# A FiLM layer on one core: one slab of 128 rows per partition instead of four of 32

## The chip, the core and the metric

The kernel runs on one core of a Trainium2 chip. The metric is the device time of one execution in microseconds, a median of several.

The engines are named as in the profile: PE multiplies matrices (PEld loads its weights), DVE is the vector engine, ACT the scalar engine, POOL is GpSimd, and SP issues DMAs and waits; DVEq or ACTq is the part of an engine that issues. The SBUF is the core's memory on the chip. A DMA is split into packets over 16 DMA engines; a completion packet of 4 bytes reports that an engine has done its part. A semaphore is the counter that such a report raises and that an instruction waits for. All times within an execution are counted from the start of the profile's span.

## The reference

```python
# x: (32, 512, 256), conditioning: (32, 64), gamma_proj, beta_proj: (64, 256), float32
gamma = conditioning @ gamma_proj
beta = conditioning @ beta_proj
return (x * (1 + gamma[:, None, :]) + beta[:, None, :]).astype(np.float32)
```

This layer scales and shifts each row by a gamma and a beta that depend on the batch. Some 16.8 MB are read, 16.8 MB are written, and each element gets one multiplication and one addition.

## The kernel before

x is cut into 4 slabs. In a slab each of the 128 partitions holds 32 consecutive rows of 256 numbers; all slabs stay in the SBUF. Loads are issued by SP, stores by ACT. The stores are held back until most loads have landed: ACT first reads one number of the last but one load (`held`, called the hold below). Of every 16 rows DVE computes 11 and POOL 5.

```python
    SLABS = 4
    BS = batch // SLABS            # batches in a slab
    REP = P // BS                  # partitions that share a batch
    ROWS = BS * seq // P           # rows per partition in a slab: 32
    x_v = x.flatten_outer_dims().rearrange("(s p r) d -> s p r d", s=SLABS, p=P)
    ...
    LOADS = {0: [8, 8, 8, 8], 3: [26, 6]}
    STORES = {0: (32,), 1: (32,), 2: (32,), 3: (16, 32)}
    GROUP = 16
    ON_DVE = 11
    ...
    nc.scalar.dma_start(out=gbproj[0::2, :], in_=gamma_proj)
    nc.scalar.dma_start(out=gbproj[1::2, :], in_=beta_proj)
    ...
    for s in range(SLABS):         # gamma and beta of a slab's 128 partitions
        for h in range(2):
            nc.tensor.matmul(p_t[:, h * dim : (h + 1) * dim],
                             lhsT=cond_T[h][:, s * P : (s + 1) * P], rhs=gbproj, ...)
        # ACT copies 1 + gamma and beta to the SBUF, for POOL
    ...
                nc.vector.scalar_tensor_tensor(out=v, in0=rows(g_p, nv), scalar=1.0, in1=v,
                                               op0=ALU.add, op1=ALU.mult)
                nc.gpsimd.tensor_tensor(out=w, in0=w, in1=rows(g_s, nw), op=ALU.mult)
                nc.vector.tensor_add(out=v, in0=v, in1=rows(b_p, nv))
                nc.gpsimd.tensor_tensor(out=w, in0=w, in1=rows(b_s, nw), op=ALU.add)
                if s == 0 and r0 + GROUP == ROWS:
                    # the hold: ACT reads a number of the last but one load before it issues any store
                    nc.scalar.copy(out=held, in_=slabs[-1][:, LOADS[SLABS - 1][0] - 1, 0:1])
                for e0, e1 in zip((0,) + STORES[s], STORES[s]):
                    if r0 < e1 <= r0 + GROUP:
                        nc.scalar.dma_start(out=o_v[s, :, e0:e1, :], in_=xs[:, e0:e1, :])
```

Of the kernel before, what the change touches and what calls it, by code (L numbers as in the profile page):

```python
# [2 lines left out]

# [5 lines left out]


@with_exitstack
def kernel(
    ctx: ExitStack,
    tc: tile.TileContext,
    x: bass.AP,
    conditioning: bass.AP,
    gamma_proj: bass.AP,
    beta_proj: bass.AP,
    out: bass.AP,  # L20
):
    nc = tc.nc
    f32 = mybir.dt.float32
    ALU = mybir.AluOpType

    batch, seq, dim = x.shape
    cond_dim = conditioning.shape[1]
    P = 128
    SLABS = 4
    BS = batch // SLABS  # L30
    REP = P // BS
    ROWS = BS * seq // P
    assert SLABS * BS == batch and REP * BS == P and ROWS * REP == seq

    x_v = x.flatten_outer_dims().rearrange("(s p r) d -> s p r d", s=SLABS, p=P)
    o_v = out.flatten_outer_dims().rearrange("(s p r) d -> s p r d", s=SLABS, p=P)

    LOADS = {0: [8, 8, 8, 8], 3: [26, 6]}
    STORES = {0: (32,), 1: (32,), 2: (32,), 3: (16, 32)}
    GROUP = 16  # L40
    ON_DVE = 11

    consts = ctx.enter_context(tc.tile_pool(name="consts", bufs=1))
    xpool = ctx.enter_context(tc.tile_pool(name="xpool", bufs=1))
    psum = ctx.enter_context(tc.tile_pool(name="psum", bufs=1, space=bass.MemoryType.PSUM))


    cond_s = consts.tile([batch, cond_dim], f32)
    nc.scalar.dma_start(out=cond_s, in_=conditioning)  # L49

    gbproj = consts.tile([2 * cond_dim, dim], f32)
    nc.scalar.dma_start(out=gbproj[0::2, :], in_=gamma_proj)  # L52
    nc.scalar.dma_start(out=gbproj[1::2, :], in_=beta_proj)

    slabs = []
    for s in range(SLABS):
        xs = xpool.tile([P, ROWS, dim], f32, name=f"xs{s}")
        slabs.append(xs)
        r = 0
        for n in LOADS.get(s, [ROWS]):  # L60
            nc.sync.dma_start(out=xs[:, r : r + n, :], in_=x_v[s, :, r : r + n, :])
            r += n
        assert r == ROWS


    ident = consts.tile([batch, batch], f32)
    make_identity(nc, ident)
    rident = consts.tile([batch, batch * REP], f32)
    nc.vector.tensor_copy(  # L69
        out=rident.rearrange("p (b g) -> p b g", g=REP),  # L70
        in_=ident.to_broadcast([batch, batch, REP]),
    )


    cond_T = []
    for h in range(2):
        wide = consts.tile([batch, cond_dim, 2], f32, name=f"wide{h}")
        nc.vector.memset(wide, 0.0)  # L78
        nc.vector.tensor_copy(out=wide[:, :, h], in_=cond_s)  # L79
        t_p = psum.tile([2 * cond_dim, batch * REP], f32, name=f"cond_T_p{h}")  # L80
        nc.tensor.matmul(t_p, lhsT=wide.rearrange("b k h -> b (k h)"), rhs=rident,  # L81
                         start=True, stop=True)
        t_s = consts.tile([2 * cond_dim, batch * REP], f32, name=f"cond_T{h}")
        nc.vector.tensor_copy(out=t_s, in_=t_p)  # L84
        cond_T.append(t_s)

    gb_p, gb_s = [], []
    for s in range(SLABS):
        p_t = psum.tile([P, 2 * dim], f32, name=f"gb_p{s}")
        for h in range(2):  # L90
            nc.tensor.matmul(p_t[:, h * dim : (h + 1) * dim],  # L91
                             lhsT=cond_T[h][:, s * P : (s + 1) * P], rhs=gbproj,
                             start=True, stop=True)
        s_t = consts.tile([P, 2 * dim], f32, name=f"gb_s{s}")
        nc.scalar.activation(out=s_t[:, :dim], in_=p_t[:, :dim],  # L95
                             func=mybir.ActivationFunctionType.Identity,
                             bias=1.0, scale=1.0)
        nc.scalar.copy(out=s_t[:, dim:], in_=p_t[:, dim:])  # L98
        gb_p.append(p_t)
        gb_s.append(s_t)  # L100

    def rows(t, n):
        return bass.AP(tensor=t.tensor, offset=t.offset, ap=[t.ap[0], [0, n], t.ap[1]])

    held = consts.tile([P, 1], f32)
    with tc.manual_schedule():
        for s in range(SLABS):
            xs = slabs[s]
            g_p, b_p = gb_p[s][:, :dim], gb_p[s][:, dim:]
            g_s, b_s = gb_s[s][:, :dim], gb_s[s][:, dim:]  # L110
            for r0 in range(0, ROWS, GROUP):
                v = xs[:, r0 : r0 + ON_DVE, :]
                w = xs[:, r0 + ON_DVE : r0 + GROUP, :]
                nv, nw = ON_DVE, GROUP - ON_DVE
                nc.vector.scalar_tensor_tensor(out=v, in0=rows(g_p, nv), scalar=1.0, in1=v,  # L115
                                               op0=ALU.add, op1=ALU.mult)
                nc.gpsimd.tensor_tensor(out=w, in0=w, in1=rows(g_s, nw), op=ALU.mult)  # L117
                nc.vector.tensor_add(out=v, in0=v, in1=rows(b_p, nv))  # L118
                nc.gpsimd.tensor_tensor(out=w, in0=w, in1=rows(b_s, nw), op=ALU.add)  # L119
                if s == 0 and r0 + GROUP == ROWS:  # L120

                    nc.scalar.copy(out=held, in_=slabs[-1][:, LOADS[SLABS - 1][0] - 1, 0:1])  # L122

                for e0, e1 in zip((0,) + STORES[s], STORES[s]):
                    if r0 < e1 <= r0 + GROUP:
                        nc.scalar.dma_start(out=o_v[s, :, e0:e1, :], in_=xs[:, e0:e1, :])
            assert STORES[s][-1] == ROWS


# [1 line left out]
_INS = ['x', 'conditioning', 'gamma_proj', 'beta_proj']  # L131
_OUTS = [((32, 512, 256), 'float32')]


# [23 lines left out]
```

## Time and profile before

| | before |
|---|---|
| time, median of the first 3 runs | 84.08 us |
| profiled span | 82.4 us |
| DVE busy, POOL busy | 51.1 us, 46.4 us |
| loads of x on q1, rest on q10, share of 16 engines | 48.3%, 48.1% |
| first DVE instruction on x, last one ends | 12.81 us, 61.9 us |
| first store issued | 41.08 us |

The lines behind this table are shown and read in the prediction below. It is enough here to see that two kinds of work share the span: arithmetic, which is over at 61.9 us, and transfers, which fill all of it.

Two lines of the timeline that the prediction uses without showing (start, duration, engine, line, operation, operands, the idle time before it and what ended it):

```profile
9.19 5.66 PE L91 MATMUL gb_p<-gbproj,cond_T 128*128 128x256 f32 x16 [0.59 <-DMA gbproj<-in_beta_proj_dram]
...
12.81 3.09 DVE L115 SCALAR_TENSOR_TENSOR xs<-gb_p,xs 128x2816 f32<-128x2816 f32 x1 [3.48 <-ACT gb_s L98]
```

The projections gate PE, and gamma and beta gate the first instruction on x.

### The profile page before, as it was taken

How to read it: one execution, taken by the hardware profiler on the slowest of the kernel's cores; microseconds unless marked ns; L12 is line 12 of the kernel's file. 1: busy time of each engine (PE TensorE's matmuls, PEld its weight loads, DVE VectorE, ACT ScalarE, POOL GpSimd, SP SyncE). 2: the span in 40 equal slices, each digit the busy share in tenths (PEclk: the TensorE clock that was granted, in tenths of full speed). 3: DMA queues.
4: the chain of work that ended last, by engine and by line, in shares of the span. 5: the costliest groups of instructions: out<-in, count | busy, mean ns of one | idle time of the engine just before them, and what ended most of it. 6: DMA issues, size and time to landing. Idle time of an engine off the chain costs nothing.

```text
span 82.4 us, 180 instructions
## 1 busy us (share of the span) xinstructions
PE 9.4 (11%) x20; PEld 5.5 (7%) x20; DVE 51.1 (62%) x23; ACT 4.1 (5%) x10; POOL 46.4 (56%) x22
## 2 busy tenths in 40 slices
PE   0069799200000000000000000000000000000000
PEld 0041478000000000000000000000000000000000
DVE  1023307999999999999999999999990000000000
ACT  0600017400000000000000000000000000000000
POOL 2000008999999999999999999999600000000000
PEclk9999999998555555555555555555555555555555
DMA  3899999979979998999797996996995999789992
GB/s 52 322 417 426 429 425 541 461 318 493 493 334 445 509 397 370 439 465 452 301 564 318 509 493 270 509 493 270 509 509 254 509 509 429 334 382 493 397 397 111
DMA packets 2080, 33.69 MB, mean 409 GB/s; under 512 B 288, under 2 KB 416, under 8 KB 544
## 3 DMA queue, kind: packets, MB, share of 16 engines
q1 hardware_dynamic: 1152, 16.78, 48.3%
q10 hardware_dynamic: 928, 16.92, 48.1%
HBM read 16.92 MB, written 16.78 MB: 409 GB/s over the span
## 4 chain that ended last, share of the span: by engine, by line
DVE 43%; issue 17%; DMA 9%; PE 4%; ACTq 1%; ACT 1%
DVE xs L115 30%; DVE xs L118 13%; DMA gbproj<-in_beta_proj_dram 9%; PE gb_p L91 4%; ACTq L52 1%; ACTq L49 0%; ACT gb_s L95 0%; ACT gb_s L98 0%
## 5 line engine op out<-in xcount | busy, mean ns | idle before, releaser
L117 POOL TENSOR_TENSOR xs<-xs,gb_s 128x1280 f32<-128x1280 f32 x8 | 23.1, 2889 | 11.5 <-ACT gb_s L95 11.5
L115 DVE SCALAR_TENSOR_TENSOR xs<-gb_p,xs 128x2816 f32<-128x2816 f32 x8 | 24.7, 3083 | 3.5 <-ACT gb_s L98 3.5
L118 DVE TENSOR_TENSOR xs<-xs,gb_p 128x2816 f32<-128x2816 f32 x8 | 24.7, 3087 | 0.3
L119 POOL TENSOR_TENSOR xs<-xs,gb_s 128x1280 f32<-128x1280 f32 x8 | 23.1, 2886 | 0.6
L91 PE MATMUL gb_p<-gbproj,cond_T 128*128 128x256 f32 x16 | 5.7, 530 | 0.6 <-DMA gbproj<-in_beta_proj_dram 0.6
L91 PEld LDWEIGHTS gb_p<-gbproj,cond_T 128*128 128x128 f32 x16 | 4.4, 280 | 3.1 <-issue 2.1
L81 PE MATMUL cond_T_p<-rident,wide 32*128 32x512 f32 x4 | 3.8, 1096 | 4.8 <-DVE rident L69 4.8
L84 DVE COPY cond_T<-cond_T_p 128x512 f32<-128x512 f32 x2 | 1.4, 692 | 3.2 <-PE cond_T_p L81 3.2
L79 DVE COPY wide<-cond_s 32x64 f32<-32x64 f32 x2 | 0.3, 182 | 3.0 <-DMA cond_s<-in_conditioning_dram 3.0
L95 ACT ACTIVATE gb_s<-gb_p 128x256 f32<-128x256 f32 x4 | 1.5, 384 | 9.3 <-PE gb_p L91 9.3
L81 PEld LDWEIGHTS cond_T_p<-rident,wide 32*128 32x128 f32 x4 | 1.2, 318 | 5.9 <-DVE rident L69 4.8
L98 ACT COPY gb_s<-gb_p 128x256 f32<-128x256 f32 x4 | 1.5, 367 | 0.0
L122 ACT COPY held<-xs 128x1 f32<-128x1 f32 x1 | 0.2, 192 | 25.3 <-DMA xs<-in_x_dram 25.3
L95 ACT ACT_TABLE_LOAD x1 | 1.3, 1283 | 2.4 <-issue 2.4
L78 DVE MEMSET wide<- 32x128 f32 x2 | 0.3, 165 | 0.8 <-PEq L142 0.8
L69 DVE COPY rident<-ident 32x512 f32<-32x512 f32 x1 | 0.4, 406 | 0.0
masks.py:197 POOL MEMSET ident<- 32x32 f32 x1 | 0.1, 114 | 0.3 <-POOLq L142 0.3
masks.py:199 POOL TENSOR_SCALAR_AFFINE_SELECT ident<-ident 32x32 f32<-32x32 f32 x1 | 0.2, 202 | 0.1
L142 POOL MEMSET const-float32-0.0<- 128x1 f32 x1 | 0.1, 104 | 0.2 <-issue 0.2
L142 POOL MEMSET const-bfloat16-1.0<- 128x1 bf16 x1 | 0.1, 107 | 0.0
L142 POOL MEMSET const-uint8-127<- 128x1 uint8 x1 | 0.1, 107 | 0.0
L142 POOL MEMSET const-float32-1.0<- 128x1 f32 x1 | 0.1, 104 | 0.0
## 6 DMA issues: line engine op xcount, KB each, us to landing
out_dram<-xs ACTq DMA_DIRECT2D x3, 4096.0 KB, 20.5
xs<-in_x_dram SPq DMA_DIRECT2D x2, 4096.0 KB, 24.6
xs<-in_x_dram SPq DMA_DIRECT2D x4, 1024.0 KB, 8.3
out_dram<-xs ACTq DMA_DIRECT2D x2, 2048.0 KB, 20.3
xs<-in_x_dram SPq DMA_DIRECT2D x1, 3328.0 KB, 35.2
xs<-in_x_dram SPq DMA_DIRECT2D x1, 768.0 KB, 35.1
gbproj<-in_gamma_proj_dram ACTq DMA_DIRECT2D x1, 64.0 KB, 6.4
gbproj<-in_beta_proj_dram ACTq DMA_DIRECT2D x1, 64.0 KB, 7.3
```

The costliest lines, as they stand in the source:

```text
L52: nc.scalar.dma_start(out=gbproj[0::2, :], in_=gamma_proj)
L69: nc.vector.tensor_copy(out=rident.rearrange("p (b g) -> p b g", g=REP), in_=ident.to_broadcast([batch, batch, REP]),)
L81: nc.tensor.matmul(t_p, lhsT=wide.rearrange("b k h -> b (k h)"), rhs=rident, start=True, stop=True)
L84: nc.vector.tensor_copy(out=t_s, in_=t_p)
L91: nc.tensor.matmul(p_t[:, h * dim : (h + 1) * dim], lhsT=cond_T[h][:, s * P : (s + 1) * P], rhs=gbproj, start=True, stop=True)
L95: nc.scalar.activation(out=s_t[:, :dim], in_=p_t[:, :dim], func=mybir.ActivationFunctionType.Identity, bias=1.0, scale=1.0)
L98: nc.scalar.copy(out=s_t[:, dim:], in_=p_t[:, dim:])
L115: nc.vector.scalar_tensor_tensor(out=v, in0=rows(g_p, nv), scalar=1.0, in1=v, op0=ALU.add, op1=ALU.mult)
L117: nc.gpsimd.tensor_tensor(out=w, in0=w, in1=rows(g_s, nw), op=ALU.mult)
L118: nc.vector.tensor_add(out=v, in0=v, in1=rows(b_p, nv))
L119: nc.gpsimd.tensor_tensor(out=w, in0=w, in1=rows(b_s, nw), op=ALU.add)
L142: nc = _bacc.Bacc("TRN2", target_bir_lowering=False, num_devices=1)
```

## The change

The intent: one slab needs only one gamma/beta pair (each partition now belongs to one batch for all its rows), the stores can be fewer and larger, and the projections come in pieces.

```diff
-    SLABS = 4
+    SLABS = 1
-    LOADS = {0: [8, 8, 8, 8], 3: [26, 6]}
-    STORES = {0: (32,), 1: (32,), 2: (32,), 3: (16, 32)}
+    LOADS = {0: [8, 8, 8, 8, 32, 32, 26, 6]}
+    STORES = {0: (64, 96, 128)}
...
-    nc.scalar.dma_start(out=gbproj[0::2, :], in_=gamma_proj)
-    nc.scalar.dma_start(out=gbproj[1::2, :], in_=beta_proj)
+    half = cond_dim // 2
+    for h, proj in enumerate((gamma_proj, beta_proj)):
+        for c0 in (0, half):
+            nc.scalar.dma_start(out=gbproj[2 * c0 + h : 2 * (c0 + half) : 2, :],
+                                in_=proj[c0 : c0 + half, :])
...
-                if s == 0 and r0 + GROUP == ROWS:
+                if s == 0 and r0 + GROUP == STORES[0][0]:
-                    nc.scalar.copy(out=held, in_=slabs[-1][:, LOADS[SLABS - 1][0] - 1, 0:1])
+                    nc.scalar.copy(out=held, in_=slabs[-1][:, ROWS - LOADS[SLABS - 1][-1] - 1, 0:1])
```

The loads keep their sizes, but a partition's rows now lie 128 KiB apart in memory from the next partition's, not 32 KiB.

## The prediction

> **What bounds the kernel now.** I read the page's slices first, then the DMA queues, then a table of windows, then the timeline. The slices already settle which resource is full:
>
> ```profile
> DVE  1023307999999999999999999999990000000000
> DMA  3899999979979998999797996996995999789992
> ...
> q1 hardware_dynamic: 1152, 16.78, 48.3%
> q10 hardware_dynamic: 928, 16.92, 48.1%
> ```
>
> The reader is to see that the vector engine stops three quarters through while the DMA row stays high from the second slice to the last but one, and that the two queues together hold 96.4% of the time of 16 engines (48.3 + 48.1). q1 is the loads of x, q10 the stores and the small inputs. The windows (columns: window, its length, PE, PEld, DVE, ACT, POOL busy, PE clock, DMA share, GB/s) say the same by stage:
>
> ```profile
> 0.00:6.00 6.00, 1.18 (x2) 0.66 (x3) 0.92 (x5) 1.28 (x1) 0.53 (x6) 1.00 0.71 261
> ...
> 24.00:30.00 6.00, 0.00 (x0) 0.00 (x0) 5.96 (x3) 0.00 (x0) 5.92 (x3) 0.50 1.00 431
> ...
> 54.00:60.00 6.00, 0.00 (x0) 0.00 (x0) 5.96 (x3) 0.00 (x0) 5.04 (x2) 0.50 1.02 437
> ...
> 66.00:72.00 6.00, 0.00 (x0) 0.00 (x0) 0.00 (x0) 0.00 (x0) 0.00 (x0) 0.50 1.01 434
> ```
>
> Loads (24 to 30) and stores (54 to 72) run at the same 431 to 437 GB/s and a DMA share of 1.0. Only the first 6 us are not full.
>
> I then added up the trace's packet records by size, per engine: 8 KiB load packets 10.44 us, 32 KiB loads 19.49, 26 KiB loads 7.94, 6 KiB loads 1.91, 32 KiB stores 29.29, 16 KiB stores 9.84, projections, conditioning and completion packets 0.55. The sum is 79.46 us. From the start of the first of these packets to the end of the last there are 79.54 us. So each of the 16 engines is busy without a gap, but for 0.1 us. The rest of the 82.4 us span is about 2.2 us before the first packet and 0.7 us after the last. The measured 84.08 us is 1.7 us more than the span.
>
> The chain of waits on the page names DVE (43%) and should not be believed here: it ends with the last DVE instruction and cannot see that the stores queue on the DMA engines. The timeline shows how far compute is from mattering:
>
> ```profile
> 34.30 3.09 DVE L118 TENSOR_TENSOR xs<-xs,gb_p 128x2816 f32<-128x2816 f32 x1
> ...
> 40.86 0.19 ACT L122 COPY held<-xs 128x1 f32<-128x1 f32 x1 [25.32 <-DMA xs<-in_x_dram]
> 41.08 21.21 ACTq L126 DMA_DIRECT2D out_dram<-xs  x5
> ...
> 58.79 3.09 DVE L118 TENSOR_TENSOR xs<-xs,gb_p 128x2816 f32<-128x2816 f32 x1
> ```
>
> The stores are held back on purpose until the 26-row load has landed (40.86). By then 64 rows per partition (four groups of 16) have been computed, at 37.4. The last result is there at 61.9, and the DMA engines reach its packets only at about 71.7 (start of the 16 KiB packets).
>
> **What the Trainium skill says.** (1) "DMA: Bandwidth & Descriptors", section "Where 436 GB/s comes from": the 16 ports at the SBUF carry 435 GB/s together. The trace agrees: a 32 KiB packet takes 1.216 to 1.218 us, which is 26.9 GB/s per engine or 431 for 16. There is almost nothing left to win in rate. (2) The same page, section "Latency and other measured facts": a copy whose rows per partition lie 512 KiB apart ran at 207 GB/s per direction, 2 MiB apart at 164, against 214 when padded. The change moves the pitch from 32 to 128 KiB, towards that but short of it. The trace has only 32 KiB, so it cannot say. (3) The same page, section "Queues, rings and completion order": each engine alternates between the queues that have work, packet by packet. The trace agrees: the projection packets (46 ns each) run between the 309 ns packets of the second load. (4) "Perfetto Trace Analysis", section "What 'DMA-bound' means": if the DMA engines themselves bind, large descriptors are what helps. The trace puts a number on that: 16 KiB take 615 ns and 32 KiB 1218, so merging two saves 12 ns.
>
> **The change, part by part.**
>
> Bytes: none change. 33.69 MB go through the same engines, so the 79.5 us stay apart from packet costs.
>
> Stores of 64, 32 and 32 rows instead of 32, 32, 32, 16 and 16. Per engine, the sixteen 16 KiB packets become eight of 32 KiB: 16 x 615 = 9.84 us become 8 x 1218 = 9.74, a saving of 0.10. The first sixteen 32 KiB packets become eight of 64 KiB if a partition's 64 KiB go as one packet: another 8 x 12 ns = 0.10 by the same cost per packet (an estimate; no 64 KiB packet has been seen). If they are cut into two, this part is 0. Completions: two fewer stores, two more inputs, 9 ns each per engine, so nothing.
>
> When stores can start: the first now needs 64 rows, ready at 37.4, and the hold releases at 40.9 anyway, so 3.5 us of slack. The second needs 96 rows (about 49.6) and its packets come up at 61.9, when the first 8 MB are through. The third needs all (61.9) and comes up at 71.7. None can run dry unless compute comes out 3.5 us later.
>
> Single gamma/beta pair: the eight logical matmuls of the projection become two, 16 PE passes of 530 ns become 4. The passes ahead of the first DVE instruction took 2.91 us and should take 4 x 0.53 = 2.1. The copies of the transposed conditioning shrink from 692 ns each to about a quarter (128 columns for 512). Three of four ACT pairs (0.38 + 0.37 us) go. All this lies before 12.8 us, beside the loads: compute starts up to 1 us earlier, and the end does not see it.
>
> Projections in two DMAs each: the ACT queue issues four instead of two, each some 0.4 to 0.6 us, so the last is issued at about 3.2 us rather than 2.3 and may land up to 1 us later than 9.05. That roughly cancels the 0.8 us above. I expect the first DVE instruction at 12 to 13 us.
>
> Load issues: the compiled order shows that the fourth load now waits for the conditioning to land (4.1 us), the fifth for the first load (5.8), the next three for gamma and beta pieces (7 to 9). They were waits in three loads before, in five now. The three loads issued at once give 3 MB, or 3.15 MB / 0.431 = 7.3 us of work, lasting to 9.5 us at least. So the fourth (issued near 4.2) and the fifth (near 6, and the fourth's 2.4 us of work lie before it) arrive in time. No gap.
>
> Pitch 128 KiB: cost unknown. I choose 0 as the middle and let it stretch the upper side: 1% on the DMA time would be 0.8 us.
>
> Sum: -0.1 to -0.2 for packets, +0.05 for longer store issue at the handover, and 0 for the rest: 84.08 - 0.15, rounded to 83.9 us.
>
> **The rivals.**
>
> (a) The larger pitch in memory slows the engines. For it: the skill's figures fall with the pitch, 16 engines walk in step, and all of x and out is affected. Against it: 512 KiB cost only about 3% (207 of 214) there, and 128 KiB is a quarter of it. If it acts, 32 KiB packets take longer than 1.22 us. A 3% loss of 78 us would be +2.3 us, 86.4 in all.
>
> (b) A store runs dry or starts late: the 64-row store is a single large step. For it: fewer, larger stores depend on more results, and all loads, arithmetic and stores now touch one tile, so a falsely wide wait would show. Against it: the compiled waits name single loads, the first arithmetic needs only two of them, and the slack is 3.5, 12 and 10 us. If compute came 5 us late, the time would grow by 1.5 us.
>
> (c) The start gets better: fewer matmuls and split projections let compute begin earlier and the kernel ends earlier. For it: PE, ACT and DVE work before 12.8 us falls by more than half. Against it: it is hidden behind 40 us of loads and the hold. Worth 0.
>
> (d) The loads starve near the start, since five issues wait now. For it: the first window is already at a share of 0.71. Against it: the queue arithmetic above leaves over 3 us. If it failed, the loss would be a microsecond or so, seen as a dip in the first slices.
>
> **Range and chances.** Packet savings can move the time by 0.2 us down and a slightly earlier or later first packet by 0.3 either way. That gives 83.4 below. Above, 1% of pitch cost gives 84.8. A gain over 2% (below 82.4) would need 1.7 us out of the 2.9 us in which the engines do not work, and nothing in the change touches these: 1%. A loss over 2% (above 85.8) needs rival (a) at full size or (b): 6%. Within 2%: 93%.
>
> **What would show it right or wrong.** Right: the two queues again at 96 to 97% of the span, 32 KiB packets at 1.22 us, the hold's copy at about 41, the first DVE instruction at 12 to 13, PE busy at about a third of 9.4 us, no dip in the slices between loads and stores. Wrong by (a): DMA share still 1.0 but GB/s below 425 in the windows of loads or stores. Wrong by (b): GB/s drops between 41 and 62 us with ACT waiting for DVE. Wrong by (d): a dip between 6 and 12 us.

## The result and the profile after

The changed kernel takes 84.11 us (median of 6 runs, 84.07 to 84.25) against 84.08 (6 runs, 84.04 to 84.35). The ratio is 1.0001, with an interval of 0.9986 to 1.0016. A second set of runs on another occasion (x11 below) gave 84.27 against 84.14, ratio 1.0022 (1.0009 to 1.0034).

The run lists show a mean granted PE clock of 0.6 for the kernel before and of 1.0 after. It does not matter here: in the windows of the kernel before the clock is 0.50 from 24 us on, and PE's last matmul ends at 14.85 us.

The slices and queues of the changed kernel:

```profile
DVE  1040007999999999999999999999990000000000
DMA  2999999799889989999999928999955995998890
...
q1 hardware_dynamic: 1152, 16.78, 48.7%
q10 hardware_dynamic: 672, 16.92, 47.8%
```

The DMA row is full again, and the queues add to 96.5%. q10 has 672 packets where it had 928. That is sixteen packets less on each of 16 engines, all from the stores; the completion packets (two stores less, two inputs more) cancel. The lone 2 in the DMA row near 48 us is not a gap. The page counts a packet whole in the slice in which it starts, and a 64 KiB packet takes 2.42 us, longer than a slice of 2.06 us; the packet records show the 16 engines busy all through that slice.

The same effect is in the windows, which the prediction wanted to use as a test:

```profile
0.00:6.00 6.00, 1.22 (x4) 0.93 (x4) 1.31 (x7) 1.28 (x1) 0.53 (x6) 1.00 0.71 263
...
24.00:30.00 6.00, 0.00 (x0) 0.00 (x0) 5.96 (x3) 0.00 (x0) 5.92 (x3) 1.00 0.98 421
...
48.00:54.00 6.00, 0.00 (x0) 0.00 (x0) 5.96 (x3) 0.00 (x0) 5.92 (x3) 1.00 0.81 350
54.00:60.00 6.00, 0.00 (x0) 0.00 (x0) 5.96 (x3) 0.00 (x0) 5.01 (x2) 1.00 1.21 524
```

421, 350 and 524 GB/s are not rates of the memory. A DMA share of 1.21 is impossible, and 350 and 524 average to 437. Here too a packet counts whole where it starts, so with packets of 32 and 64 KiB even a window of 6 us is off by what crosses its edges. The durations of single packets are the measure: the 32 KiB loads take 1216 ns in both kernels.

The timeline of the changed kernel, at the points that were shown of the kernel before:

```profile
10.04 2.04 PE L94 MATMUL gb_p<-gbproj,cond_T 128*128 128x256 f32 x4 [4.37 <-DMA gbproj<-in_beta_proj_dram]
...
12.80 3.09 DVE L118 SCALAR_TENSOR_TENSOR xs<-gb_p,xs 128x2816 f32<-128x2816 f32 x1 [6.80 <-ACT gb_s L101]
...
34.29 3.09 DVE L121 TENSOR_TENSOR xs<-xs,gb_p 128x2816 f32<-128x2816 f32 x1
...
40.95 0.19 ACT L125 COPY held<-xs 128x1 f32<-128x1 f32 x1 [28.18 <-DMA xs<-in_x_dram]
41.19 21.10 ACTq L129 DMA_DIRECT2D out_dram<-xs  x3
...
58.78 3.09 DVE L121 TENSOR_TENSOR xs<-xs,gb_p 128x2816 f32<-128x2816 f32 x1
```

PE starts 0.85 us later, as the projections land later, and is done sooner. The first DVE instruction is at 12.80 for 12.81: the two cancel to 0.01 us. Everything after it stands within 0.1 us of where it stood before.

The packet records, summed per engine, in us:

| | before | after |
|---|---|---|
| 8 KiB loads (first four) | 10.44 | 10.67 |
| other loads | 29.33 | 29.33 |
| stores | 39.14 | 38.87 |
| first packet's start to last packet's end | 79.55 | 79.34 |

So the stores did get cheaper by 0.27 us, and the first loads dearer by 0.22. One run of each cannot settle tenths; the two profiled executions themselves took 84.25 and 84.07 us. The experiments take this up.

### The profile page after: what moved, and what is told of

Its sections match the earlier page's. It is cut to its first block, busy times and chain, and to the rows that moved or that the text cites. A ratio compares the mean times of both kernels' runs of the same rounds, so it can differ in the third digit from the quotient of the medians.

```text
span 82.3 us, 140 instructions
## 1 busy us (share of the span) xinstructions
PE 3.3 (4%) x8; PEld 2.1 (3%) x8; DVE 50.1 (61%) x23; ACT 2.1 (3%) x4; POOL 46.4 (56%) x22
## 4 chain that ended last, share of the span: by engine, by line
DVE 52%; DMA 8%; issue 8%; ACTq 3%; PE 2%; ACT 1%
DVE xs L118 30%; DVE xs L121 23%; DMA gbproj<-in_beta_proj_dram 8%; PE gb_p L94 2%; ACTq L55 2%; ACTq L49 0%; ACT gb_s L98 0%; ACT gb_s L101 0%
## 5 line engine op out<-in xcount | busy, mean ns | idle before, releaser
L94 PE MATMUL gb_p<-gbproj,cond_T 128*128 128x256 f32 x4 | 2.0, 666 | 4.4 <-DMA gbproj<-in_beta_proj_dram 4.4
L84 PE MATMUL cond_T_p<-rident,wide 32*128 32x128 f32 x4 | 1.2, 456 | 4.5 <-DVE rident L72 4.5
L94 PEld LDWEIGHTS gb_p<-gbproj,cond_T 128*128 128x128 f32 x4 | 1.2, 323 | 4.8 <-issue 4.6
L87 DVE COPY cond_T<-cond_T_p 128x128 f32<-128x128 f32 x2 | 0.6, 292 | 1.0 <-PE cond_T_p L84 0.9
L98 ACT ACTIVATE gb_s<-gb_p 128x256 f32<-128x256 f32 x1 | 0.4, 383 | 7.1 <-PE gb_p L94 7.1
L101 ACT COPY gb_s<-gb_p 128x256 f32<-128x256 f32 x1 | 0.4, 367 | 0.0
```

The lines of the kernel that those rows point to most:

```text
L84: nc.tensor.matmul(t_p, lhsT=wide.rearrange("b k h -> b (k h)"), rhs=rident, start=True, stop=True)
L87: nc.vector.tensor_copy(out=t_s, in_=t_p)
L94: nc.tensor.matmul(p_t[:, h * dim : (h + 1) * dim], lhsT=cond_T[h][:, s * P : (s + 1) * P], rhs=gbproj, start=True, stop=True)
L98: nc.scalar.activation(out=s_t[:, :dim], in_=p_t[:, :dim], func=mybir.ActivationFunctionType.Identity, bias=1.0, scale=1.0)
L101: nc.scalar.copy(out=s_t[:, dim:], in_=p_t[:, dim:])
```

## The experiments

### What sets the end: arithmetic or transfers

**Half of the arithmetic taken away** (wrong result):

```diff
-                nc.vector.tensor_add(out=v, in0=v, in1=rows(b_p, nv))
-                nc.gpsimd.tensor_tensor(out=w, in0=w, in1=rows(b_s, nw), op=ALU.add)
```

> The changed kernel without the additions of beta on both engines (the result is wrong on purpose): half of the arithmetic is gone, the vector engine busy falls from 50.1 to about 25 us. My theory: no change, 84.1 us, as the hold and the DMA engines set the end. Rival (arithmetic is on the path): faster by several us.

Measured: 84.24 us against 84.13, ratio 1.0012 (0.9997 to 1.0027). The page shows DVE with gaps and the DMA row as full as before:

```profile
DVE  1040007992059930899199900000000000000000
DMA  3799999699799899999999909999956995998990
```

DVE is busy 25.7 us instead of 50.1 and the time does not fall. The rival that puts arithmetic on the path is dead, and with it the reading of the page's chain, which gives DVE 52% of the changed kernel's span.

**More rows on DVE**, to use up the margin:

```diff
-    ON_DVE = 11
+    ON_DVE = 12        # x3: in the changed kernel;  14 in x1 (changed kernel) and x2 (kernel before)
```

> The changed kernel with 12 of 16 rows on the vector engine: an instruction of about 3.36 us. My theory: 64 rows ready at 12.8 + 8 x 3.38 = 39.9, still ahead of the hold at 40.95, all rows at 66.9 ahead of 71.7 - 1.35: no change, 84.1 us. Rival (the compute chain sets the end): 4.5 us more, 88.6.

> The changed kernel with 14 instead of 11 of 16 rows on the vector engine: a vector instruction grows from 3.08 to about 3.92 us. My theory (the DMA engines bind, compute has a margin that the 64-row first store has shrunk to 3.5 us): 64 rows ready at 12.8 + 8 x 3.95 = 44.4 instead of 37.4, first store packets at about 45.8, a hole of some 3.2 us; all rows ready at 76.0, the last store's packets start at about 77.3 instead of 71.7 and the time is 77.3 + 9.75 + 0.65 + 1.75 = 89.4 us. Rival (compute has ample margin in the new kernel as in the old one): about 85.

> The kernel before with 14 of 16 rows on the vector engine. My theory: the 32-row first store is ready at 28.6, the second at 44.4 (its turn comes at 52), the fourth at 68 (its turn: 71.7), the last 16 rows at 76.0 plus 1.35 us to the first packet, against a turn at 76.6: a hole of 0.8 us, so 84.9 us. Rival (the vector engine's chain, which the page names first, sets the end): 13 us more in both kernels, about 97.

Measured, all against 84.13 us: 12 rows, 84.25 us, ratio 1.0016 (1.0002 to 1.0031), not told from the changed kernel's own 1.0001 and 1.0022; 14 rows in the changed kernel, 88.55 us, ratio 1.0534 (1.0517 to 1.0552); 14 rows in the kernel before, 84.15 us, ratio 1.0001 (0.9986 to 1.0016). The timeline of the changed kernel with 14 rows:

```profile
39.97 3.89 DVE L121 TENSOR_TENSOR xs<-xs,gb_p 128x3584 f32<-128x3584 f32 x1
41.11 0.19 ACT L125 COPY held<-xs 128x1 f32<-128x1 f32 x1 [28.27 <-DMA xs<-in_x_dram]
...
43.93 0.37 ACTq L129 DMA_DIRECT2D out_dram<-xs  x1
```

And of the kernel before with 14 rows:

```profile
39.71 3.89 DVE L118 TENSOR_TENSOR xs<-xs,gb_p 128x3584 f32<-128x3584 f32 x1
40.88 0.19 ACT L122 COPY held<-xs 128x1 f32<-128x1 f32 x1 [25.06 <-DMA xs<-in_x_dram]
...
41.10 2.91 ACTq L126 DMA_DIRECT2D out_dram<-xs  x2
```

Both have the same DVE instructions at nearly the same times. In the kernel before, ACT issues the first store 0.22 us after the hold's start, as its 32 rows were long ready. In the changed kernel it waits for the instruction that ends at 43.86 and issues at 43.93. The windows (DMA share and GB/s are the last two columns) of the changed kernel, then of the kernel before, hint at the loss:

```profile
40.00:42.50 2.50, 0.00 (x0) 0.00 (x0) 2.50 (x1) 0.19 (x1) 1.27 (x1) 1.00 0.77 315
42.50:45.00 2.50, 0.00 (x0) 0.00 (x0) 2.50 (x2) 0.00 (x0) 2.49 (x2) 1.00 0.98 419
...
74.20:76.20 2.00, 0.00 (x0) 0.00 (x0) 0.55 (x1) 0.00 (x0) 0.00 (x0) 1.00 0.61 262
```

```profile
40.00:42.50 2.50, 0.00 (x0) 0.00 (x0) 2.50 (x1) 0.19 (x1) 1.43 (x2) 0.50 1.22 510
42.50:45.00 2.50, 0.00 (x0) 0.00 (x0) 2.50 (x2) 0.00 (x0) 2.42 (x3) 0.50 0.99 419
...
74.20:76.20 2.00, 0.00 (x0) 0.00 (x0) 0.29 (x1) 0.00 (x0) 0.00 (x0) 0.50 1.10 467
```

They cannot place it. In the kernel before, the first store packets start within the first of these windows and count whole there; in the changed kernel they start just before 45.0 and count whole in the second, which so hides the hole that it contains. The packet records are the evidence. In the changed kernel the last load packet ends at 42.51 and the first store packet starts at 44.81, a hole of 2.3 us. A second one, of 1.6 us, lies between 74.07 and 75.67, where the last store of 32 rows waits for the last instruction. In the profiled run of the kernel before, the engines go from loads to stores without a hole.

What follows: the margin is real, and the change has cut it. The loss was about 4.45 us (4.49 by the ratio, 0.0534 x 84.13, and 4.42 by the medians) where 5.3 were expected, and the kernel before lost nothing where 0.8 were expected. Both misses have mainly one cause: DVE instructions follow each other every 3.87 us, not 3.95, so the last result came some 1.25 us earlier than expected (1.5 us in the kernel before). The time is only 0.85 us below the expectation, so other terms of that sum were some 0.4 us too small. I had scaled the whole duration by rows and added a gap, while an instruction here may start just before the one ahead ends (39.97 + 3.89 = 43.86, the next starts at 43.77).

### Do packets cost what was assumed

**The two 32-row loads cut into sixteen of 4 rows:**

```diff
-    LOADS = {0: [8, 8, 8, 8, 32, 32, 26, 6]}
+    LOADS = {0: [8] * 4 + [4] * 16 + [26, 6]}
```

> The changed kernel with the two 32-row loads cut into sixteen of 4 rows: 112 more packets per engine. My theory (12 ns for each packet more, on the path, as packets fill the engines): 112 x 12 = 1.34 us plus 14 more completions of 9 ns = 0.13, so 85.6 us, with 4 KiB packets of about 163 ns. Rival (packet cost overlaps or is not on the path): 84.1.

Measured: 85.43 us against 84.06, ratio 1.0168 (1.0147 to 1.0189), that is +1.41 us. The records: 4 KiB packets take 162 ns, and those loads sum to 20.84 us per engine instead of 19.48, or +1.36; completions go from 0.07 to 0.20. Sum +1.49. Set against the changed kernel's own two ratios, 1.0001 and 1.0022, the time is 1.23 to 1.40 us longer. So packet cost is on the path, nearly one for one, at 12 ns a packet. (The interval is clear of 1.)

**The old stores in the changed kernel:**

```diff
-    STORES = {0: (64, 96, 128)}
+    STORES = {0: (32, 64, 96, 112, 128)}
```

> The changed kernel with the stores of the kernel before (32, 32, 32, 16, 16 rows). My theory: 16 more packets per engine, +0.2 us, within the scatter of the runs; the DMA stretch in the trace 79.5 instead of 79.3 us. Rival (the 64-row store hid a loss from the larger pitch, and both cancelled): slower by 0.5 us or more.

Measured: 84.47 us against 84.06, ratio 1.0051 (1.0037 to 1.0064), +0.43 us. Against the kernel before, that is twice the expectation and short of the rival's 0.5; against the changed kernel's own two ratios it is 0.24 to 0.42 us. It has the same data packets as the kernel before, so something in the change costs about 0.4 us, and the larger stores give part of it back. This is what the remaining runs were for.

### Which part costs, which part gives back

**Each projection in one DMA again**, with the new stores (x7), with the old stores (x9, the slab part alone), and the split alone in the kernel before (x10):

```diff
-    for h, proj in enumerate((gamma_proj, beta_proj)):
-        for c0 in (0, half):
-            nc.scalar.dma_start(out=gbproj[2 * c0 + h : 2 * (c0 + half) : 2, :],
-                                in_=proj[c0 : c0 + half, :])
+    nc.scalar.dma_start(out=gbproj[0::2, :], in_=gamma_proj)
+    nc.scalar.dma_start(out=gbproj[1::2, :], in_=beta_proj)
     # x9 also: STORES = {0: (32, 64, 96, 112, 128)};  x10: the reverse edit in the kernel before
```

> The changed kernel with each projection in one DMA again. My theory: the projections land about 0.9 us earlier (near 9.05), the first vector instruction starts near 11.9 instead of 12.8, and the time does not change: 84.1 us. Rival (the start of compute carries to the end): 83.2.

> One slab with the old stores and each projection in one DMA: the slab part alone. The run with the old stores and split projections came out 0.4 us slower than the kernel before, where packets explain nothing (both have the same packets). Theory A (the slab and its larger pitch cost nothing): 84.1. Theory B (the pitch costs some 0.35 us, which the fewer stores give back): 84.4, with a longer DMA stretch or longer packets. Theory C (the split projections cost it): 84.1.

> The kernel before with the projections split in two DMAs each: that part alone. Theory A and B: 84.1, though the first vector instruction starts about 0.9 us later. Theory C (the split projections and the later load issues they bring cost 0.3 to 0.4 us): 84.4.

> The changed kernel itself, unedited, on the chip of these runs, as the measure for the parts: my theory 84.1 and a ratio within 0.2% of 1. If the parts cancel (theory B or C), it still is 84.1, but a part alone is not.

| run | slab | stores | projections | median us, this / before | ratio (95%) |
|---|---|---|---|---|---|
| x9 | one | old | one DMA | 84.20 / 84.14 | 1.0011 (0.9999 to 1.0024) |
| x7 | one | new | one DMA | 84.02 / 84.06 | 0.9997 (0.9984 to 1.0010) |
| x10 | four | old | split | 84.61 / 84.14 | 1.0061 (1.0048 to 1.0073) |
| x6 | one | old | split | 84.47 / 84.06 | 1.0051 (1.0037 to 1.0064) |
| x11 | one | new | split | 84.27 / 84.14 | 1.0022 (1.0009 to 1.0034) |

x6 and x7 ran with x5 and x8 beside one set of runs of the kernel before; x9 to x12 beside another. Every split row is above its unsplit partner: 0.0061 over the kernel before itself, 0.0040 (x6 over x9), 0.0025 (x11 over x7). The last of these is the weakest: with the changed kernel's first ratio, 1.0001, it would be 0.0004. The slab alone is not told from zero. The new stores take off 0.0014 (x9 to x7, within the intervals) and 0.0029 (x6 to x11). Theory C holds: the split costs. Theory B falls: the slab and its pitch alone cost at most 0.0024, or 0.2 us, where it asked for 0.35.

x7 also shows that an earlier start of compute is worth nothing by itself:

```profile
8.98 2.04 PE L91 MATMUL gb_p<-gbproj,cond_T 128*128 128x256 f32 x4 [3.17 <-DMA gbproj<-in_beta_proj_dram]
...
11.75 3.09 DVE L115 SCALAR_TENSOR_TENSOR xs<-gb_p,xs 128x2816 f32<-128x2816 f32 x1 [5.60 <-ACT gb_s L98]
```

DVE starts 1.05 us earlier than in the changed kernel, and the ratio differs by 0.0004 from the first measurement of that kernel and by 0.0025 from the second, in which the split's own cost lies. The 83.2 us of the rival are not there.

Where the split's cost sits, from the packet records. First, the time of the four 8-row loads, summed per engine, in us (eight packets of 8 KiB each):

```
                        load 1  load 2  load 3  load 4
one DMA:  before          3.01    2.47    2.47    2.49
          x7              2.89    2.48    2.47    2.48
          x9              3.05    2.47    2.47    2.49
split:    after           2.96    2.52    2.67    2.52
          x11             2.97    2.53    2.67    2.52
          x10             3.06    2.54    2.66    2.52
          x6              2.77    2.54    2.66    2.52
```

Load 1 scatters with how the engines start. Loads 2 to 4 do not: 7.43 or 7.44 us in each unsplit run, 7.70 to 7.72 in each split one, and the other traces with these loads agree (x2, unsplit: 7.43; x1, x3, x4 and x5, split: 7.69 to 7.72). That is 0.28 us on every engine, on the path. The packets of load 3 take a median of 325 to 334 ns instead of 309. The bytes and the number of data packets are the same. Why they are slower I did not find out. The records place the slowness: in the changed kernel the packets that start from 5.0 to 6.5 us take 309 ns, those between 6.5 and 9.5 us 317 to 356 (means of half microseconds), later ones some 315; the projection packets run from 5.2 to 9.1 us. Running between projection packets is not enough for it, as in the unsplit runs the load packets beside them, from 5.0 to 8.3 us, take 309 to 314. What differs beside the DMAs themselves is that SP issues only the first three loads at once, where it issued five, and the last of the others after pieces of the projections. In x5 SP issues loads until 27 us, and its 4 KiB packets take 172 ns at most, so an issue as such does not slow packets either. What does stays open.

Second, the end of the program. SP waits for the completion of all DMAs there. The summary of its waits, for the kernel before and then for x6 (total us, times, longest):

```profile
SPq L153 <- DMA out_dram<-xs: 38.7, 5, 9.7
```

```profile
SPq L156 <- DMA out_dram<-xs: 48.6, 1, 48.6
```

The kernel before goes through the stores' completions one after another as they come, and the last store's is the last of its list. x6 meets the last store's semaphore early in its list and sits on it for 48.6 us; when it comes, the others, long fulfilled, are still to be gone through. The instruction records, as us after the end of the last packet (in x10 and x6 the wait for the last store itself began 40 us earlier, ended at 0.37 and 0.35, and is not listed):

```
                DMAs   SP's waits at           then drains at
before           16    0.35                    0.41
after            16    0.40                    0.46
x11 (after)      16    0.40                    0.47
x9               16    0.35                    0.42
x7               14    0.36 0.43 0.49          0.55
x12              13    0.35 0.41 0.47 0.53     0.60
x10              18    0.41 0.47 0.53 0.59     0.66
x6               18    0.39 0.45 0.51 0.57     0.64
```

Each instruction takes 0.06 us and covers up to two semaphores. The DMA instructions of these programs name eight semaphores, in turn. With 16 DMAs the last store has the last of the eight, and no instruction is left after its own; with 18 it has the second, and four are left. By the last column that is 0.25 us for x10 over the kernel before and 0.22 for x6 over x9. So x10 and x6 pay 0.28 + 0.25 = 0.53 and 0.28 + 0.22 = 0.50 us for the split, against the measured 0.51 (0.0061 x 84.14) of x10 and 0.34 between x9 and x6. (In x6's one profiled execution load 1 happened to be as much faster as loads 2 to 4 were slower, so its whole DMA stretch, 79.57 us, does not show the 0.28 against x9's 79.64.) The changed kernel pays the 0.28 and only 0.05 at the end, because its two fewer stores bring the number of DMAs back to 16, and saves some 0.2 to 0.27 on store packets. That is the cancellation.

### A version with fewer packets

**Two attempts to win the packet cost back**, the first with the split, the second without:

```diff
-    LOADS = {0: [8, 8, 8, 8, 32, 32, 26, 6]}
+    LOADS = {0: [8, 24, 32, 32, 26, 6]}          # x8
+    LOADS = {0: [8, 8, 16, 32, 32, 26, 6]}       # x12, each projection in one DMA
```

> The changed kernel with loads of 8, 24, 32, 32, 26 and 6 rows: 16 fewer packets per engine and two fewer completions. My theory: 16 x 12 = 0.19 us less, 83.9, at the edge of what the runs resolve; the first vector instruction as before if rows 8 to 31 land near 12.3. Rival: the first group of rows lands later and nothing is gained, 84.1.

> One slab, the three stores, each projection in one DMA, and the third and fourth 8-row loads joined to one of 16 rows, behind the projections: 8 packets fewer per engine than with four 8-row loads. My theory: 8 x 12 = 0.1 us less than with the loads of 8, so 83.9 to 84.0, no hole before the stores since compute starts near 11.8. The gain is at the limit of what the runs resolve. Rival: the 16-row load comes late for the second group and a hole appears.

Measured for x8: 87.69 us against 84.06, ratio 1.0432 (1.0418 to 1.0446). A clear miss of mine. Its timeline:

```profile
17.35 2.05 PE L94 MATMUL gb_p<-gbproj,cond_T 128*128 128x256 f32 x4 [11.62 <-DMA gbproj<-in_beta_proj_dram]
...
20.11 3.09 DVE L118 SCALAR_TENSOR_TENSOR xs<-gb_p,xs 128x2816 f32<-128x2816 f32 x1 [14.05 <-ACT gb_s L101]
```

The projections, which take 46 ns a packet, now alternate with load packets of 24 KiB, 920 ns each (from 12.3 us on of 32 KiB, 1216 ns), instead of 8 KiB, 309 ns. They reach PE at 17.35 instead of 10.04 us. Compute starts at 20.11, 7.3 us later, which is more than the 3.5 us of margin. The first store packet starts at 45.65 where the last load packet ended at 42.34: a hole of 3.3 us, and that is nearly all of the loss. I had thought of when rows 8 to 31 land, not of what the small inputs have to queue behind.

Measured for x12: 84.15 us against 84.14, ratio 1.0009 (0.9995 to 1.0023). Its DMA stretch is 79.25 us, the shortest of all, but its 13 DMAs leave four wait instructions at the end. No gain that the runs can resolve. No version here beats the kernel before.

## Why the prediction was right

83.9 us were predicted, 84.11 and then 84.27 measured, inside the range of 83.4 to 84.8; "within 2%" was given 0.93. Point by point:

- **The transfers are the bound.** Shown: half the arithmetic gone changes nothing (x4), 112 packets more per engine cost what they add (x5).
- **Store packets, 0.1 to 0.2 us less.** The 64 KiB do go as one packet, of 2420 ns median against 2 x 1218. The stores fell from 39.14 to 38.87 us, 0.27.
- **Compute has 3.5 us of slack ahead of the first store.** Shown from both sides: 12 rows on DVE fit (x3), 14 do not (x1), and x8 breaks it from the start of compute. Rival (b) was the right danger, and the change brought it nearer without setting it off.
- **Fewer matmuls and later projections cancel before 12.8 us.** 2.04 us of PE as estimated, 0.85 us later; DVE at 12.80. Rival (c) is worth nothing (x7). Two sizes were off without effect: the last piece of the projections was issued by 3.74 us instead of 3.2, and the copies of the transposed conditioning shrank from 692 to 292 ns, not to a quarter.
- **The larger pitch costs 0.** 1216 ns for a 32 KiB load packet in both kernels, and x9 within 0.0024 of 1. Rival (a) is refuted for 128 KiB. My test for it, "GB/s below 425 in the windows", was badly chosen: the window from 24 to 30 us shows 421 while its packets take the same 1216 ns.
- **The loads do not starve (rival d).** From 2 to 12 us the packets add up to the whole time of 16 engines. But here is the term that was mis-sized: the step "Projections in two DMAs each" and the one on load issues ended in "no gap", and so in no cost. There is indeed no gap, yet the packets of loads 2 to 4 grow by 0.28 us in sum.
- **The sum of -0.15 us.** Its sign was wrong by a little: 0.2 to 0.27 saved on stores, 0.28 lost in the split, and the two measurements of the ratio, 1.0001 and 1.0022, average to +0.1 us. "Completions: nothing" was right for packets and missed the waits at the program's end, which this change hardly touches (0.05 us) as it happens to keep 16 DMAs. So the bound and the margins were foreseen, but that the sum came so close to zero was luck: a saving that was counted met a cost that was not.
- **Readings of the trace.** The prediction counts its packet times from a start that lies some 0.5 us before the timeline's. On the timeline's clock the first packet starts at 1.73 us, not 2.2, the last ends 1.16 us before the span does, not 0.7, and the 16 KiB stores start at 71.18, not 71.7; the slack of the second and third store is 0.5 us less than stated. The same shift is in the expectations of x1 to x3, where the 1.35 us to a first packet are 0.9, and the 0.65 us after the last are 1.16. Nothing that was concluded hangs on it. The "1.7 us more than the span" set the median against a profile of an execution of 84.25 us; run for run it is 1.8.

## What to carry to other kernels

When the packets of all DMA engines fill the span without a gap, as they do here, only bytes, packets and the first and last microseconds count; work taken off the compute engines only moves margin, and a change should be judged by how much margin it leaves (here 14 rows on DVE cost the new kernel 5% and the old one nothing). A null result may be two small effects that cancel: undo the parts one at a time before calling each of them free. And put small inputs that gate the start behind small packets only.

## What the Trainium skill lacked or had wrong

- "DMA: Bandwidth & Descriptors", section "Latency and other measured facts": the figures for row pitch start at 512 KiB. Here 32 and 128 KiB give the same 1216 ns for 32 KiB packets.
- The same page, section "Why small descriptors are slow": it has a cost of some 3 cycles in the engine's bus and of 32 bytes of metadata, and calls packing worthwhile only up to 256 bytes. Here larger packets (not packing, which no run tried) still paid: 112 more per engine, of 4 KiB (162 ns) instead of 32 KiB (1216 ns), cost 1.41 us (1.36 in the packet records), some 12 ns each, and one of 64 KiB (2420 ns) takes 16 ns less than two of 32 KiB.
- The same page, section "Queues, rings and completion order": it says that an engine alternates by packets, and lacks the consequence for small inputs: behind 920 ns packets the projections came 7.3 us later than behind 309 ns ones.
- No page that I read has the waits at the end of such a program: 0.06 us for every two semaphores that are left after the last store's, none to four such instructions here.
- No page that I read explains why 8 KiB load packets took 325 to 334 ns instead of 309 beside the split projections.
